# Expert stage: order of the gate eviction's access, one gate group moved from ACT to DVE, row rates, last squares added on DVE

## The chip, the cores and the metric

The kernel runs on one core of a Trainium2 chip. Its engines work side by side, each on its own queue in order: PE (TensorE, matrix products), DVE (VectorE), ACT (ScalarE), POOL (GpSimd) and SP (it only issues DMA transfers). They wait for one another through semaphores. The metric is the device time of one execution in microseconds (us); lower is better.

## The reference, cut to what matters

Two transformer blocks run one after the other on 512 tokens of width 1024. The change touches the last part of the first block, a mixture of 16384 experts:

```python
def block(xb):                       # 128 tokens
    q = (xb @ w_q).reshape(PEER_BLOCK, PEER_HEADS, 2, PEER_QDIM // 2)
    s = jnp.einsum('thsd,hsnd->thsn', q, sub_keys)
    sv, si = lax.top_k(s, PEER_TOPK)
    ...
    top, pos = lax.top_k(cand, PEER_TOPK)
    e = jnp.take_along_axis(cidx, pos, axis=-1)   # 8 heads x 16 experts a token
    g = jax.nn.softmax(top, axis=-1)
    act = jax.nn.gelu(jnp.einsum('thkd,td->thk', u_tab[e], xb), approximate=False)
    return jnp.einsum('thk,thkd->td', g * act, v_tab[e])
```

Each token uses 128 of the 16384 rows of the up-table `u_tab` and the down-table `v_tab`. The result is added to the block's `h`, and the next block begins with a root-mean-square norm of `h`.

## The kernel before, in words

Products are done in full fp32 precision as three products of two-part operands (`mm3`, L167 to L169): high times high, high times low, low times high. Weights come in blocks of 1 MB (`wload`) and are cut into halves of 1024 columns; `halves` makes the high part on ACT (L119, tile `whi`) and the low part on DVE by a subtraction (L120, tile `wlo`). Activations are split in the same way: L161 on ACT and L162 on DVE with a gain, L158 and L159 without.

The expert stage (`experts`) treats the tokens in two ways.

- The first 128 tokens fetch their own table rows. `gathered` is a generator of steps: an indirect DMA on POOL's queue (L1005) fetches one row for each of 128 tokens, 0.52 MB, and one DVE instruction works on an earlier row: a dot product with a row of the up-table (`dot`, L1010) or a weighted addition of a row of the down-table (`add`, L1021). There are 256 rows. `some(n)` takes n such steps on average; `RATE` holds n for the first 28 units, for the other units, and for each half of a down-table block. Each step is tied to a recent matrix product, so that it doesn't run ahead of PE.
- The other 384 tokens multiply with the whole tables. `unit(b)` loads one block of the up-table (b from 0 to 63), runs 48 products of 384 columns each three times, and evicts with the Gelu on ACT (L1252). Sixty units stand in a first loop; their results go to DRAM (`act_dram`).

Beside the units of the first loop runs `side`, a generator whose parts are taken up by cost (`DUE` for each unit): `select` (choice of experts, on DVE) and `gates`. `gates` makes, for 16 tokens at a time, a tile `st` with the gate of every expert. A group is four tokens. It needs a one-hot matrix `ga` scaled by the gate and a one-hot matrix `gb` (L1212, DVE). For three of four groups `ga` is a comparison on DVE (L1202) and four scalings on ACT (L1204); for the fourth it is four Abs (L1207) and four Relu (L1209) on ACT. Four matrix products (L1190) give a PSUM tile of four tokens by 128, and `finish` evicts it on ACT into `st` (L1191). A full tile goes to DRAM (`gate_dram`).

A second loop runs over 16 blocks c of four units, in the order 0, 15, 1 to 14. `read` fetches the activations of a block from DRAM, or `evaluate` runs the last four units for block 15. `weigh` loads the gates (L1283, tile `gt`, POOL's queue) and multiplies them in on DVE (L1287, tile `wt`), with a split by L158 and L159. `combine` multiplies with the down-table of the block before. So `evaluate(15)` and `weigh(15)` are issued ahead of the first `combine`: this place is called "between the tables" below. After the last block `done(m)` splits `h` for the next stage and adds up its squares (`sq_add`: a Square on ACT, an addition L200 on POOL).

The order of each engine's queue is set by a scheduler from this program; nothing is written out by hand.

Of the kernel before, what the change touches and what calls it, by code (L numbers as in the profile page):

```python
# [15 lines left out]
AF = mybir.ActivationFunctionType  # L16
ALU = mybir.AluOpType
# [5 lines left out]
T = 512  # L23
# [16 lines left out]
ON_POOL = (2, 3, 4, 5, 6, 7)  # L40
GATHERED = 128
PACE, PACE_D, AHEAD_G = 2, 4, 1
RATE = (0.9, 2.6, 2.2)
OHB, UGB = 1, 6
ULAG = 1
FIRST, STEP = (6, 3, 3), (1, 1, 1)
# [6 lines left out]
class Kern:  # L53
# [130 lines left out]
        return y  # L184


    def sq_add(self, acc, src, first, n=T, eng=None):
        nc = self.nc
        if eng is not None and first:
            eng.tensor_mul(acc[:, :n], src, src)  # L190
        elif eng is not None:
            sq = self.t(self.sp, [P, T], "sq")
            eng.tensor_mul(sq[:, :n], src, src)
            nc.gpsimd.tensor_add(acc[:, :n], acc[:, :n], sq[:, :n])
        elif first:
            nc.scalar.activation(acc[:, :n], src, AF.Square)
        else:
            sq = self.t(self.sp, [P, T], "sq")
            nc.scalar.activation(sq[:, :n], src, AF.Square)  # L199
            nc.gpsimd.tensor_add(acc[:, :n], acc[:, :n], sq[:, :n])  # L200

    def acc_rstd(self, acc, width, n=T):
        nc = self.nc
# [779 lines left out]
    def experts(self, ctx):  # L983


        nc, A, tc, gv = self.nc, self.A, self.tc, self.gv
# [61 lines left out]
        def some(n):  # L1048
            pace.append(self.last_mm)
            credit[0] += n  # L1050
            while credit[0] >= 1:
                credit[0] -= 1
                next(rows, None)

        with tc.tile_pool(name="pa", bufs=1) as sp_, ExitStack() as es:
# [22 lines left out]
            with tc.tile_pool(name="pq", bufs=2) as qp:  # L1078
                rb = self.bcast(self.norm()[1](), qp, "rb")
                for k in range(KD):  # L1080
                    t = self.t(qp, [P, T], "xt", bufs=KD)
# [102 lines left out]
            def gates(tt):  # L1184
                late = []

                def finish(st, t0, a, bs):
                    ps = self.ps()
                    for i in range(4):
                        nc.tensor.matmul(ps[:, i * P:(i + 1) * P], bs[:, i, :], a[:, i, :], start=True, stop=True)  # L1190
                    nc.scalar.activation(st[:, :, t0:t0 + 4].rearrange("p i t -> p t i"), ps.rearrange("p (t i) -> p t i", t=4), AF.Copy)  # L1191

                for tb in range(max(tt * P - G, 0) // TG, (tt * P + P - G) // TG):
                    st = self.t(ap, [P, P, TG], "st", bufs=2)
                    for t0 in range(0, TG, 4):
                        t = tb * TG + t0
                        a = self.t(ap, [P, 4, P], "ga", bufs=LAG + 2)
                        four = lambda n: picks[n][:, t:t + 4, None].to_broadcast([P, 4, P])
                        rows4 = iota[:, None, :].to_broadcast([P, 4, P])

                        if t0 // 4 % 4 != 3:
                            nc.vector.tensor_tensor(a, rows4, four(0), op=ALU.is_equal)  # L1202
                            for i in range(4):
                                nc.scalar.activation(a[:, i, :], a[:, i, :], AF.Copy, scale=picks[2][:, t + i:t + i + 1])  # L1204
                        else:
                            for i in range(4):
                                nc.scalar.activation(a[:, i, :], iota, AF.Abs, bias=picks[0][:, t + i:t + i + 1], scale=-1.0)  # L1207
                            for i in range(4):
                                nc.scalar.activation(a[:, i, :], a[:, i, :], AF.Relu, bias=picks[2][:, t + i:t + i + 1],  # L1209
                                                     scale=picks[3][:, t + i:t + i + 1])  # L1210
                        bs = self.t(ap, [P, 4, P], "gb", bufs=LAG + 1)
                        nc.vector.tensor_tensor(bs, rows4, four(1), op=ALU.is_equal)  # L1212
                        late.append((st, t0, a, bs, tb))
                        if len(late) > LAG:
                            z = late.pop(0)
                            finish(*z[:4])
                            if z[1] == TG - 4:
                                nc.scalar.dma_start(gate_d[z[4]], z[0].rearrange("p i t -> p (i t)"))
                        yield GCOST[tt]
                for z in late:  # L1220
                    finish(*z[:4])
                    if z[1] == TG - 4:
                        nc.scalar.dma_start(gate_d[z[4]], z[0].rearrange("p i t -> p (i t)"))
                    yield 0.1
# [30 lines left out]
            while b < 60 or b < 64 and work is not None or b % 4:  # L1255
# [11 lines left out]
                if room:  # L1267
                    some(RATE[0 if b < 28 else 1])
            for _ in work or ():
                pass  # L1270
        first = b // 4
        with tc.tile_pool(name="pb", bufs=2) as ap:
            def slots():
                while True:
                    yield self.t(ap, [P, D], "ug", bufs=UGB)
            room["u"] = slots()

            def weigh(c, acts, pool, tag):

                W = []  # L1280
                for b0 in range(0, 8, 4):
                    gt = self.t(ap, [P, N // TG, 4, TG], "gt", bufs=3)
                    nc.gpsimd.dma_start(gt.rearrange("p b i t -> p b (i t)"),  # L1283
                                        gate_d[:, :, (c * 8 + b0) * TG:(c * 8 + b0 + 4) * TG].rearrange("b j c -> j b c"))
                    for b in range(b0, b0 + 4):
                        w = self.t(ap, [P, N], "wt", bufs=2)
                        nc.vector.tensor_mul(w.rearrange("p (b t) -> p b t", t=TG), acts(b).rearrange("p (b t) -> p b t", t=TG), gt[:, :, b - b0, :])  # L1287
                        h, l = self.split(w, n=N, tag=tag, pool=pool, bufs=8)
                        W.append((h[:, :N], l[:, :N]))
                return W  # L1290

            acc = []

            def combine(c, W, begin, end):

                for dh in range(2):
                    if end and dh == 0:
                        for _ in rows:
                            pass
                    if begin:  # L1300
                        acc.extend(self.ps()[:, :N] for _ in range(4))
                    for sub in range(2):
                        v = self.wload(A["peer_v"][c, dh, sub])
                        for e0 in range(0, 4, 2):
                            for d in range(4):
                                for e in range(e0, e0 + 2):
                                    k = sub * 4 + e
                                    self.mm3(acc[dh * 4 + d], v(e * 512 + d * P, e * 512 + (d + 1) * P), W[k], begin and k == 0, end and k == 7)
                        if end and dh == 1 and sub == 0:
                            for k0 in (0, 4):  # L1310
                                gathered_out(k0)
                            for m in range(4):
                                self.done(m)
                        some(RATE[2])
                    if end:
                        for m in range(dh * 4, dh * 4 + 4):
                            nc.vector.tensor_add(self.hT[m][:, G:], acc[m], self.hT[m][:, G:])
                            if dh == 1:
                                self.done(m)

            def read(c):
                ac = [self.t(ap, [P, 2, 2, N], "ac", bufs=3) for _ in range(2)]
                for b in range(2):
                    nc.gpsimd.dma_start(ac[b].rearrange("p b a t -> p b (a t)"), act_d[c * 4 + 2 * b:c * 4 + 2 * b + 2].rearrange("b j c -> j b c"))
                return ac

            def evaluate(c):
                ac = [self.t(ap, [P, 2, 2, N], "ac", bufs=3) for _ in range(2)]
                for b in range(4):
                    unit(c * 4 + b, ac[b // 2][:, b % 2])  # L1330
                    some(RATE[1])
                return ac


            order, W = [0, *range(first, 16), *range(1, first)], None
            for i, c in enumerate(order):
                ac = evaluate(c) if c >= first else read(c)
                W2 = weigh(c, lambda b: ac[b // 4][:, b % 4 // 2, b % 2, :], *((self.xp, "x") if i % 2 else (ap, "w")))
                if W is not None:
                    combine(order[i - 1], W, i == 1, False)  # L1340
                W = W2
            combine(order[-1], W, False, True)


# [551 lines left out]
```

## Time and profile before

| quantity | value |
|---|---|
| median of three runs | 4026.0 us (4025.2 to 4029.67) |
| the profiled execution, its own time | 4027.37 us |
| span of its trace, first to last instruction | 4025.5 us |
| mean granted clock of PE | 0.983 |
| busy, share of the span | PE 97%, DVE 61%, ACT 43%, POOL 19% |

The span is 1.9 us shorter than the time of that execution. [...] The expert stage lies at about 495 to 1856 us: the query product up to 610, the units without gates to about 735, units with gates to 1258, the place between the tables to about 1292, the down-table to 1836, and then the next stage, whose first instructions overlap with its end.

### The profile page before, as it was taken

To read this page: it belongs to the slowest core of one execution; us is meant where nothing else is said; L and a number is where in the kernel's file an instruction comes from. 1 tells how busy PE (TensorE), PEld (TensorE's weight loads), DVE (VectorE), ACT (ScalarE), POOL (GpSimd) and SP (SyncE) were. 2 spreads that over 40 slices of the span, in tenths; PEclk is the share of its full clock that TensorE was granted. 3 is DMA by queue.
4 is the path that set the end of the run, shared out by engine and by line. 5 is a ranking of instruction groups with operands and counts; after the bars stand their busy time and mean duration, and the time that the engine had idled before them with its cause. 6 is when DMAs were issued, how large, how long until landed. Compare 5 with 4: busy or idle time off the path is not lost.

```text
span 4025.5 us, 52157 instructions
## 1 busy us (share of the span) xinstructions
PE 3903.0 (97%) x20105; PEld 3426.6 (85%) x20105; DVE 2466.5 (61%) x4683; ACT 1730.9 (43%) x3040; POOL 745.9 (19%) x704
## 2 busy tenths in 40 slices
PE   7999999899998999999999999999999999999999
PEld 6878789899988999998888778888888888888887
DVE  7666459988766788876444575643444447665443
ACT  3445434567774333333223365532332236654222
POOL 7401100122323555542000101000000011010000
PEclk8989999999998999999999999999999999999999
DMA  4214225578977999983223211222222232032232
GB/s 138 69 37 136 74 74 177 202 269 289 329 273 273 359 385 357 355 311 128 97 97 101 92 43 63 85 91 102 92 102 99 95 97 69 32 105 74 89 105 79
DMA packets 130042, 608.27 MB, mean 151 GB/s; under 512 B 22320, under 2 KB 25568, under 8 KB 89472
## 3 DMA queue, kind: packets, MB, share of 16 engines
q1 hardware_dynamic: 55296, 362.96, 25.6%
q0 software_dynamic: 48672, 185.73, 13.1%
q10 hardware_dynamic: 25824, 56.23, 3.9%
q8 instruction: 158, 2.59, 0.3%
q14 instruction: 92, 0.75, 0.1%
HBM read 551.92 MB, written 52.95 MB: 150 GB/s over the span
## 4 chain that ended last, share of the span: by engine, by line
PE 80%; DVE 11%; ACT 3%; DMA 2%; issue 1%; POOL 1%; SPq 0%; ACTq 0%; DVEq 0%; POOLq 0%
PE ps_ffn L168 12%; PE ps_ffn L167 12%; PE ps_ffn L169 12%; PE ps_peer L169 7%; PE ps_peer L167 7%; PE ps_peer L168 7%; PE ps_mixer L168 2%; PE ps_mixer L167 2%; PE ps_mixer L169 2%; DVE wlo_peer L120 2%; PE ps_peer L1190 1%; DMA gt_peer<-gate_dram 1%; PE ps_xm L167 1%; PE ps_mem L167 1%; PE ps_xm L169 1%
## 5 line engine op out<-in xcount | busy, mean ns | idle before, releaser
L119 ACT ACTIVATE whi_ffn<-wraw_ffn 128x1024 fp32r<-128x1024 f32 (+2 forms) x304 | 278.7, 944 | 924.2 <-PE ps_ffn L168 906.4
L167 PE MATMUL ps_peer<-xh_peer,whi_peer 128*128 128x384 f32 (+1 forms) x1664 | 578.0, 348 | 28.2 <-ACT whi_peer L119 26.0
L169 PE MATMUL ps_peer<-xh_peer,wlo_peer 128*128 128x384 f32 (+1 forms) x1664 | 570.9, 344 | 12.5 <-DVE wlo_peer L120 12.2
L168 PE MATMUL ps_peer<-xl_peer,whi_peer 128*128 128x384 f32 (+1 forms) x1664 | 570.7, 343 | 0.0
L119 ACT ACTIVATE whi_peer<-wraw_peer 128x1024 fp32r<-128x1024 f32 x272 | 286.1, 1056 | 435.1 <-PE ps_peer L168 409.6
L120 DVE TENSOR_TENSOR wlo_ffn<-wraw_ffn,whi_ffn 128x1024 fp32r<-128x1024 f32 (+2 forms) x304 | 331.0, 1090 | 180.6 <-ACT whi_ffn L119 179.9
L120 DVE TENSOR_TENSOR wlo_peer<-wraw_peer,whi_peer 128x1024 fp32r<-128x1024 f32 x272 | 330.2, 1222 | 120.3 <-ACT whi_peer L119 104.3
L331 DVE TENSOR_TENSOR g_ffn<-ps_ffn,rb_ffn 128x512 f32<-128x512 f32 x88 | 60.8, 691 | 480.4 <-PE ps_ffn L169 480.4
L167 PEld LDWEIGHTS ps_peer<-xh_peer,whi_peer 128*128 128x128 f32 x1664 | 318.2, 191 | 38.1 <-ACT whi_peer L119 30.9
L169 PEld LDWEIGHTS ps_peer<-xh_peer,wlo_peer 128*128 128x128 f32 x1664 | 317.5, 191 | 22.4 <-DVE wlo_peer L120 16.8
L168 PEld LDWEIGHTS ps_peer<-xl_peer,whi_peer 128*128 128x128 f32 x1664 | 318.0, 191 | 4.7
L167 PE MATMUL ps_ffn<-xh_xm,whi_ffn 128*128 128x512 f32 x704 | 274.2, 390 | 0.0
L169 PE MATMUL ps_ffn<-xh_xm,wlo_ffn 128*128 128x512 f32 x704 | 273.9, 389 | 0.0
L168 PE MATMUL ps_ffn<-xl_xm,whi_ffn 128*128 128x512 f32 x704 | 273.9, 389 | 0.0
L167 PE MATMUL ps_ffn<-ah_ffn,whi_ffn 128*128 128x512 f32 x704 | 273.9, 389 | 0.0
L168 PE MATMUL ps_ffn<-al_ffn,whi_ffn 128*128 128x512 f32 x704 | 273.9, 389 | 0.0
L169 PE MATMUL ps_ffn<-ah_ffn,wlo_ffn 128*128 128x512 f32 x704 | 273.9, 389 | 0.0
L200 POOL TENSOR_TENSOR sqacc_ffn<-sqacc_ffn,sq_ffn 128x512 f32<-128x512 f32 x21 | 30.6, 1456 | 1039.3 <-ACT sq_ffn L199 1033.1
L169 PE MATMUL ps_peer<-wh_peer,wlo_peer 128*128 128x384 f32 x512 | 171.9, 338 | 14.0 <-DVE wlo_peer L120 14.0
L167 PE MATMUL ps_peer<-wh_peer,whi_peer 128*128 128x384 f32 x512 | 171.7, 335 | 0.0
L168 PE MATMUL ps_peer<-wl_peer,whi_peer 128*128 128x384 f32 x512 | 171.6, 335 | 0.0
L1005 POOL DMA_INDIRECT ug_peer<-in_peer_v_rows_dram,idx_peer x85 | 135.9, 1598 | 128.0 <-DVE accg_peer L1021 59.2
(762 smaller groups left out, 9258.8 us busy)
## 6 DMA issues: line engine op xcount, KB each, us to landing
wraw_ffn<-in_ffn_gu_dram SPq DMA_DIRECT2D x88, 1024.0 KB, 4.7
wraw_peer<-in_peer_u_dram SPq DMA_DIRECT2D x64, 1024.0 KB, 5.6
wraw_peer<-in_peer_v_dram SPq DMA_DIRECT2D x64, 1024.0 KB, 8.1
wraw_ffn<-in_ffn_dn_dram SPq DMA_DIRECT2D x64, 704.0 KB, 4.0
gate_dram<-st_peer ACTq DMA_DIRECT2D x24, 1024.0 KB, 7.4
gt_peer<-gate_dram POOLq DMA_DIRECT2D x32, 768.0 KB, 11.2
act_dram<-at_peer ACTq DMA_DIRECT2D x60, 384.0 KB, 4.3
ac_peer<-act_dram POOLq DMA_DIRECT2D x30, 768.0 KB, 8.6
```

Source lines behind the costliest of these rows:

```text
L119: nc.scalar.activation(hi[:, :m], raw, AF.Copy)
L120: nc.vector.tensor_sub(lo[:, :m], raw, hi[:, :m].bitcast(F32))
L167: nc.tensor.matmul(ps, a[0], b[0], start=first, stop=False)
L168: nc.tensor.matmul(ps, a[0], b[1], start=False, stop=False)
L169: nc.tensor.matmul(ps, a[1], b[0], start=False, stop=last)
L200: nc.gpsimd.tensor_add(acc[:, :n], acc[:, :n], sq[:, :n])
L331: nc.vector.tensor_mul(g, pg, rb)
L1005: nc.gpsimd.indirect_dma_start(out=u, out_offset=None, in_=A[table], in_offset=bass.IndirectOffsetOnAxis(ap=idx[:, s:s + 1], axis=0))
L1190: nc.tensor.matmul(ps[:, i * P:(i + 1) * P], bs[:, i, :], a[:, i, :], start=True, stop=True)
```

## The change

Five edits, all in the expert stage.

- `RATE` goes from (0.9, 2.6, 2.2) to (0.6, 3.0, 2.3): fewer rows in the first 28 units, more in the others and in the down-table.
- The gate eviction in `finish` copies the same 128x512 elements, but runs through them in the order of its target. Before, it read PSUM in order and wrote each element 64 bytes from the one before; now it writes `st` in runs of four elements and reads PSUM in steps of 512 bytes.
- For the second and third gate sets (`tt` over 1), the fourth group's `ga` is made on DVE by a comparison and a multiplication instead of eight instructions on ACT.
- `evaluate` takes no rows.
- At the end of the stage, `done` doesn't add the squares; `sq_add` does it after the splits of each half, with the addition on DVE.

```diff
--- before.py
+++ after.py
@@ -40,7 +40,7 @@
 ON_POOL = (2, 3, 4, 5, 6, 7)
 GATHERED = 128
 PACE, PACE_D, AHEAD_G = 2, 4, 1
-RATE = (0.9, 2.6, 2.2)
+RATE = (0.6, 3.0, 2.3)
 OHB, UGB = 1, 6
 ULAG = 1
 FIRST, STEP = (6, 3, 3), (1, 1, 1)
@@ -184,20 +184,21 @@
         return y
 
 
-    def sq_add(self, acc, src, first, n=T, eng=None):
+    def sq_add(self, acc, src, first, n=T, eng=None, add=None):
         nc = self.nc
+        add = add or nc.gpsimd
         if eng is not None and first:
             eng.tensor_mul(acc[:, :n], src, src)
         elif eng is not None:
             sq = self.t(self.sp, [P, T], "sq")
             eng.tensor_mul(sq[:, :n], src, src)
-            nc.gpsimd.tensor_add(acc[:, :n], acc[:, :n], sq[:, :n])
+            add.tensor_add(acc[:, :n], acc[:, :n], sq[:, :n])
         elif first:
             nc.scalar.activation(acc[:, :n], src, AF.Square)
         else:
             sq = self.t(self.sp, [P, T], "sq")
             nc.scalar.activation(sq[:, :n], src, AF.Square)
-            nc.gpsimd.tensor_add(acc[:, :n], acc[:, :n], sq[:, :n])
+            add.tensor_add(acc[:, :n], acc[:, :n], sq[:, :n])
 
     def acc_rstd(self, acc, width, n=T):
         nc = self.nc
@@ -1188,7 +1189,7 @@
                     ps = self.ps()
                     for i in range(4):
                         nc.tensor.matmul(ps[:, i * P:(i + 1) * P], bs[:, i, :], a[:, i, :], start=True, stop=True)
-                    nc.scalar.activation(st[:, :, t0:t0 + 4].rearrange("p i t -> p t i"), ps.rearrange("p (t i) -> p t i", t=4), AF.Copy)
+                    nc.scalar.activation(st[:, :, t0:t0 + 4], ps.rearrange("p (t i) -> p i t", t=4), AF.Copy)
 
                 for tb in range(max(tt * P - G, 0) // TG, (tt * P + P - G) // TG):
                     st = self.t(ap, [P, P, TG], "st", bufs=2)
@@ -1198,7 +1199,10 @@
                         four = lambda n: picks[n][:, t:t + 4, None].to_broadcast([P, 4, P])
                         rows4 = iota[:, None, :].to_broadcast([P, 4, P])
 
-                        if t0 // 4 % 4 != 3:
+                        if tt > 1 and t0 // 4 % 4 == 3:
+                            nc.vector.tensor_tensor(a, rows4, four(0), op=ALU.is_equal)
+                            nc.vector.tensor_mul(a, a, four(2))
+                        elif t0 // 4 % 4 != 3:
                             nc.vector.tensor_tensor(a, rows4, four(0), op=ALU.is_equal)
                             for i in range(4):
                                 nc.scalar.activation(a[:, i, :], a[:, i, :], AF.Copy, scale=picks[2][:, t + i:t + i + 1])
@@ -1310,13 +1314,16 @@
                             for k0 in (0, 4):
                                 gathered_out(k0)
                             for m in range(4):
-                                self.done(m)
+                                self.done(m, False)
+                                self.sq_add(self.acc, self.hT[m], m == 0, add=nc.vector)
                         some(RATE[2])
                     if end:
                         for m in range(dh * 4, dh * 4 + 4):
                             nc.vector.tensor_add(self.hT[m][:, G:], acc[m], self.hT[m][:, G:])
                             if dh == 1:
-                                self.done(m)
+                                self.done(m, False)
+                        for m in range(4 * dh, 8 * dh):
+                            self.sq_add(self.acc, self.hT[m], False, add=nc.vector)
 
             def read(c):
                 ac = [self.t(ap, [P, 2, 2, N], "ac", bufs=3) for _ in range(2)]
@@ -1328,7 +1335,6 @@
                 ac = [self.t(ap, [P, 2, 2, N], "ac", bufs=3) for _ in range(2)]
                 for b in range(4):
                     unit(c * 4 + b, ac[b // 2][:, b % 2])
-                    some(RATE[1])
                 return ac
```

On ACT, in the later units with gates, the rows of one stretch before (L1191 is the eviction, L1204 the scaling, L1207 and L1209 the fourth group, L1252 the Gelu):

```order
L1191 ACTIVATE st_peer_9640<-ps_peer_10045 128x4x128
L1258 DMA act_dram<-at_peer_9972 128x768
L1191 ACTIVATE st_peer_9640<-ps_peer_10067 128x4x128
L1191 ACTIVATE st_peer_10036<-ps_peer_10082 128x4x128
L1218 DMA gate_dram<-st_peer_9640 128x2048
L1204 ACTIVATE ga_peer_10074<-ga_peer_10074,pick_peer_5180 128x128 x4
L1252 ACTIVATE at_peer_10097<-ps_peer_10108 128x384
L1207 ACTIVATE ga_peer_10161<-iota_peer_5176,pick_peer_5178 128x128 x4
L1209 ACTIVATE ga_peer_10161<-ga_peer_10161,pick_peer_5180,pick_peer_5181 128x128 x4
L1204 ACTIVATE ga_peer_10192<-ga_peer_10192,pick_peer_5180 128x128
```

And the matching stretch of the changed kernel, where L1192 is the eviction and L1208 the scaling:

```order
L1192 ACTIVATE st_peer_9601<-ps_peer_10006 128x128x4
L1262 DMA act_dram<-at_peer_9933 128x768
L1192 ACTIVATE st_peer_9601<-ps_peer_10028 128x128x4
L1192 ACTIVATE st_peer_9997<-ps_peer_10043 128x128x4
L1222 DMA gate_dram<-st_peer_9601 128x2048
L1208 ACTIVATE ga_peer_10035<-ga_peer_10035,pick_peer_5180 128x128 x4
L1256 ACTIVATE at_peer_10058<-ps_peer_10069 128x384
L1208 ACTIVATE ga_peer_10147<-ga_peer_10147,pick_peer_5180 128x128 x4
L119 ACTIVATE whi_peer_10179<-wraw_peer_10173 128x1024
L119 ACTIVATE whi_peer_10288<-wraw_peer_10286 128x1024
```

The eviction has its two inner dimensions exchanged, and the eight instructions of the fourth group are gone, so that a copy of weights (L119) follows the scalings.

On DVE, between the tables, the last twelve rows up to the first subtraction for the down-table, `wlo_peer_12026`; L1010 and L1021 are the row instructions:

```order
L159 TENSOR_TENSOR wl_peer_11679<-wt_peer_11676,wh_peer_11678 128x384
L1021 SCALAR_TENSOR_TENSOR accg_peer_4356<-ug_peer_11749,act_peer_4359,accg_peer_4356 128x1024
L1010 SCALAR_TENSOR_TENSOR ug_peer_11752,hid_peer_4358<-ug_peer_11752,xg_peer_4355 128x1024
L1021 SCALAR_TENSOR_TENSOR accg_peer_4356<-ug_peer_11817,act_peer_4359,accg_peer_4356 128x1024
L1010 SCALAR_TENSOR_TENSOR ug_peer_11820,hid_peer_4358<-ug_peer_11820,xg_peer_4355 128x1024
L1021 SCALAR_TENSOR_TENSOR accg_peer_4356<-ug_peer_11885,act_peer_4359,accg_peer_4356 128x1024
L1015 TENSOR_TENSOR act_peer_4359<-act_peer_4359,g_peer_4360 128x16
L1010 SCALAR_TENSOR_TENSOR ug_peer_11890,hid_peer_4358<-ug_peer_11890,xg_peer_4355 128x1024
L1021 SCALAR_TENSOR_TENSOR accg_peer_4356<-ug_peer_11893,act_peer_4359,accg_peer_4356 128x1024
L1010 SCALAR_TENSOR_TENSOR ug_peer_11958,hid_peer_4358<-ug_peer_11958,xg_peer_4355 128x1024
L1021 SCALAR_TENSOR_TENSOR accg_peer_4356<-ug_peer_11961,act_peer_4359,accg_peer_4356 128x1024
L120 TENSOR_TENSOR wlo_peer_12026<-wraw_peer_12023,whi_peer_12025 128x1024
```

The same place in the changed kernel, where the multiplication is L1291 and the first subtraction for the down-table is `wlo_peer_11918`:

```order
L159 TENSOR_TENSOR wl_peer_11588<-wt_peer_11585,wh_peer_11587 128x384
L159 TENSOR_TENSOR wl_peer_11594<-wt_peer_11591,wh_peer_11593 128x384
L1291 TENSOR_TENSOR wt_peer_11597<-ac_peer_11554,gt_peer_11583 128x384
L1291 TENSOR_TENSOR wt_peer_11603<-ac_peer_11554,gt_peer_11583 128x384
L159 TENSOR_TENSOR wl_peer_11600<-wt_peer_11597,wh_peer_11599 128x384
L1291 TENSOR_TENSOR wt_peer_11861<-ac_peer_11609,gt_peer_11859 128x384
L120 TENSOR_TENSOR wlo_peer_11918<-wraw_peer_11915,whi_peer_11917 128x1024
L159 TENSOR_TENSOR wl_peer_11606<-wt_peer_11603,wh_peer_11605 128x384
L1291 TENSOR_TENSOR wt_peer_11867<-ac_peer_11609,gt_peer_11859 128x384
L120 TENSOR_TENSOR wlo_peer_11922<-wraw_peer_11915,whi_peer_11921 128x1024
```

No row instruction stands ahead of the subtraction any more; the first multiplication of block 15, which needs the gate tile `gt_peer_11859`, does. On POOL's queue the loads of `gt_peer_11859` and its neighbour now follow the loads for block 0 at once, where eleven row transfers stood before them.

On DVE, at the end of the stage, before (L162 splits `h`, L1317 adds the expert result to `h`, `wlo_ffn` belongs to the next stage):

```order
L162 SCALAR_TENSOR_TENSOR xl_peer_16940<-h_91,gains,xh_peer_16939 128x512
L1317 TENSOR_TENSOR h_92<-ps_peer_12151,h_92 128x384
L120 TENSOR_TENSOR wlo_ffn_3191_17048<-wraw_ffn_3187_17041,whi_ffn_3190_17047 128x1024
L162 SCALAR_TENSOR_TENSOR xl_peer_17006<-h_92,gains,xh_peer_17005 128x512
L1317 TENSOR_TENSOR h_93<-ps_peer_12152,h_93 128x384
L1317 TENSOR_TENSOR h_94<-ps_peer_12153,h_94 128x384
L1317 TENSOR_TENSOR h_95<-ps_peer_12154,h_95 128x384
L120 TENSOR_TENSOR wlo_ffn_3200_17124<-wraw_ffn_3198_17121,whi_ffn_3199_17123 128x1024
L162 SCALAR_TENSOR_TENSOR xl_peer_17014<-h_93,gains,xh_peer_17013 128x512
L162 SCALAR_TENSOR_TENSOR xl_peer_17022<-h_94,gains,xh_peer_17021 128x512
L162 SCALAR_TENSOR_TENSOR xl_peer_17030<-h_95,gains,xh_peer_17029 128x512
```

And in the changed kernel, where L1322 adds the result and L201 adds the squares:

```order
L162 SCALAR_TENSOR_TENSOR xl_peer_16844<-h_91,gains,xh_peer_16843 128x512
L201 TENSOR_TENSOR sqacc_peer_16823<-sqacc_peer_16823,sq_peer_16847 128x512
L1322 TENSOR_TENSOR h_92<-ps_peer_12046,h_92 128x384
L1322 TENSOR_TENSOR h_93<-ps_peer_12047,h_93 128x384
L120 TENSOR_TENSOR wlo_ffn_3189_16948<-wraw_ffn_3187_16945,whi_ffn_3188_16947 128x1024
L162 SCALAR_TENSOR_TENSOR xl_peer_16910<-h_92,gains,xh_peer_16909 128x512
L162 SCALAR_TENSOR_TENSOR xl_peer_16915<-h_93,gains,xh_peer_16914 128x512
L1322 TENSOR_TENSOR h_94<-ps_peer_12048,h_94 128x384
L1322 TENSOR_TENSOR h_95<-ps_peer_12049,h_95 128x384
L201 TENSOR_TENSOR sqacc_peer_16823<-sqacc_peer_16823,sq_peer_16928 128x512
L162 SCALAR_TENSOR_TENSOR xl_peer_16920<-h_94,gains,xh_peer_16919 128x512
L162 SCALAR_TENSOR_TENSOR xl_peer_16925<-h_95,gains,xh_peer_16924 128x512
```

Two additions of squares stand among these rows, and the second subtraction for the next stage now comes after the last split instead of before the split of `h_92`.

## Rows read from the trace of the kernel before

**Rows 1.** Windows: microseconds, then busy time (and instructions) of each engine, clock, DMA.
```profile
735.00:921.00 186.00, 173.30 (x1047) 170.95 (x1047) 167.97 (x479) 130.56 (x265) 39.57 (x26) 0.96 0.69 242
921.00:1258.00 337.00, 314.00 (x1910) 309.68 (x1909) 236.66 (x301) 245.14 (x505) 91.08 (x70) 0.96 0.80 286
1258.00:1312.00 54.00, 41.95 (x229) 41.20 (x228) 34.74 (x49) 17.12 (x29) 27.58 (x23) 0.87 0.89 319
1312.00:1415.00 103.00, 97.36 (x555) 95.77 (x554) 83.04 (x119) 37.54 (x53) 54.82 (x39) 1.00 0.94 355
750.00:850.00 100.00, 90.92 (x552) 89.17 (x551) 99.42 (x342) 70.86 (x140) 14.56 (x8) 0.97 0.56 195
```

**Rows 2.** PE's waits in the windows of rows 1 and 1835–1870: total, times, longest.
```profile
PE ps_peer L169 <- DVE wlo_peer L120: 6.1, 4, 2.0
PE ps_peer L167 <- ACT whi_peer L119: 4.9, 1, 4.9
...
PE ps_peer L167 <- ACT whi_peer L119: 20.3, 10, 5.0
...
PE ps_peer L169 <- DVE wlo_peer L120: 12.0, 1, 12.0
...
PE ps_peer L169 <- DVE wlo_peer L120: 4.8, 3, 2.1
...
PE ps_ffn L168 <- DVE xl_peer L162: 3.2, 2, 2.5
```

**Rows 3.** Timeline of ACT before one gap: start, length, instructions.
```profile
1219.21 1.60 ACT L1209 ACTIVATE ga_peer<-ga_peer,pick_peer,pick_peer 128x128 f32<-128x128 f32 x4
...
1221.54 1.25 ACT L1204 ACTIVATE ga_peer<-ga_peer,pick_peer 128x128 f32<-128x128 f32 x4
...
1223.53 2.00 ACT L119 ACTIVATE whi_peer<-wraw_peer 128x1024 fp32r<-128x1024 f32 x2
```

**Rows 4.** Timeline of PE after that gap: first, 16th and 26th step.
```profile
1224.64 0.69 PE L167 MATMUL ps_peer<-xh_peer,whi_peer 128*128 128x384 f32 x1 [4.83 <-ACT whi_peer L119]
...
1229.91 0.39 PE L169 MATMUL ps_peer<-xh_peer,wlo_peer 128*128 128x384 f32 x1
...
1231.71 0.33 PE L168 MATMUL ps_peer<-xl_peer,whi_peer 128*128 128x384 f32 x1
```

**Rows 5.** Groups of ACT by line, 921–1258: busy time, mean ns, idle before.
```profile
L1191 ACT ACTIVATE st_peer<-ps_peer 128x512 f32<-128x512 f32 x65 | 68.9, 1078 | 4.7 <-ACT st_peer L1191 2.1 <-PE ps_peer L1190 1.4 <-ACT ga_peer L1207 0.2
...
L1209 ACT ACTIVATE ga_peer<-ga_peer,pick_peer,pick_peer 128x128 f32<-128x128 f32 x64 | 26.8, 483 | 0.0
L1207 ACT ACTIVATE ga_peer<-iota_peer,pick_peer 128x128 f32<-128x128 f32 x64 | 20.3, 388 | 0.0
```

**Rows 6.** The contiguous copy L1105: ns (shortest, median, longest), first and last start.
```profile
L1105 ACT ACTIVATE xn_peer<-ps_peer x16: 577/582/622, 516.9 to 608.6; 128x512 f32<-128x512 f32 x16
```

**Rows 7.** Groups of DVE by line, 921–1258, as rows 5.
```profile
L1021 DVE SCALAR_TENSOR_TENSOR accg_peer<-sc_peer,act_peer,accg_peer 128x1024 f32<-128x1024 f32 x38 | 48.7, 1281 | 38.3 <-PE ps_peer L169 38.2
L1010 DVE SCALAR_TENSOR_TENSOR sc_peer<-sc_peer,xg_peer 128x1024 f32<-128x1024 f32 x37 | 45.2, 1222 | 28.6 <-PE ps_peer L169 28.6
L1212 DVE TENSOR_TENSOR gb_peer<-iota_peer,pick_peer 128x512 f32<-128x512 f32 x62 | 42.3, 690 | 1.8 <-PE ps_peer L1190 1.8
```

**Rows 8.** Timeline of DVE between the tables: first, last row instruction, subtractions after.
```profile
1288.29 1.22 DVE L1010 SCALAR_TENSOR_TENSOR ug_peer<-ug_peer,xg_peer 128x1024 f32<-128x1024 f32 x1
...
1301.62 1.28 DVE L1021 SCALAR_TENSOR_TENSOR accg_peer<-ug_peer,act_peer,accg_peer 128x1024 f32<-128x1024 f32 x1 [0.60 <-DMA ug_peer<-in_peer_v_rows_dram,idx_peer]
1302.82 2.35 DVE L120 TENSOR_TENSOR wlo_peer<-wraw_peer,whi_peer 128x1024 fp32r<-128x1024 f32 x2
```

**Rows 9.** DVE's waits in 1258–1312.
```profile
DVE wt_peer L1287 <- DMA gt_peer<-gate_dram: 7.1, 1, 7.1
```

**Rows 10.** The split L162 in other stages and at this end, as rows 6.
```profile
L162 DVE SCALAR_TENSOR_TENSOR xl_ffn<-h,gains,xh_ffn x24: 744/747/747, 2161.9 to 3314.0; 128x512 fp32r<-128x512 f32 x24
...
L162 DVE SCALAR_TENSOR_TENSOR xl_peer<-h,gains,xh_peer x8: 740/1756/1780, 1838.9 to 1854.6; 128x512 fp32r<-128x512 f32 x8
```

## Prediction

> **What bounds the kernel now.** I read the table of windows first, because the change touches only the expert stage, and a share over the whole kernel would say little about it. In that table the reader is to compare PE's busy time with the length of its window [rows 1]. PE is busy for nearly all of each window, so a shorter time can come only from PE's idle time and from the time that its clock was at the lower of its two levels. In 921 to 1258 us, the stretch in which gate tiles are made beside the up-table, PE is idle for 337 − 314.0 = 23.0 us at a mean granted clock of 0.96. In 735 to 921 us it is idle for 12.7 us, also at 0.96. Between the two tables (1258 to 1312) it is idle for 12.1 us at 0.87, and in the first part of the down-table (1312 to 1415) for 5.6 us at 1.00.
>
> The waits of PE say who ended these gaps [rows 2]. In 921 to 1258 it is ACT's copy of the weights, L119 (20.3 us in 10 waits). In 735 to 921 it is that copy (4.9) and DVE's subtraction L120 (6.1). Between the tables one wait on L120 takes all 12.0 us, three more take 4.8 in the next window, and at the stage's end two waits on the split L162 take 3.2.
>
> ACT is busy for only 245 of the 337 us, so it is late in bursts, not on the whole. The timeline before one such gap shows a burst [rows 3]: four L1209 (1.60 us), four L1204 (1.25), with evictions between, and the copy L119 that PE waits for begins at 1223.53, behind all of them. PE starts again at 1224.64 after 4.83 us, and then runs slowly: 15 steps to 1229.91 take 5.27 us, 0.35 each, and the next ten to 1231.71 take 0.18 each [rows 4]. [...]
>
> **The change part by part.** The sum is made against the profiled execution, 4027.4 us, which is 1.4 above the median of the three.
>
> *ACT in the gate stage.* In 921 to 1258 ACT ran 64 L1207 (20.3 us) and 64 L1209 (26.8 us), that is 16 groups of four tokens, and 65 gate evictions L1191 of 1078 ns [rows 5]. All of these 16 groups go to DVE: −47.1 us. The eviction has 128x512 elements on either side of the change; what changes is which side has gaps, the write before and the PSUM read after. No row shows a read of PSUM with gaps. The bounds are 0.58 us, the same size copied with no gaps by L1105 [rows 6], and 1.08, that the read costs what the write did. I take 0.60: both ends are rows of the same engine, size and source, and the one difference of L1191 from L1105 is its pattern. Where the runs of four now lie in the write, the write is near to L1105's. That is 65 × 0.48 = −31 us. ACT then works 245 − 47 − 31 = 167 us, half of the window, and the burst of [rows 3] shrinks by the 1.6 us of L1209, as much of L1207 before it, and 0.48 for each of its evictions.
>
> [...]
>
> How much PE wins: the idle 20.3 us, and the time lost at the low clock. For the latter the clock gives bounds: 0.04 × 337 × 2 = 27 us at the lower level, of which between 23 (every idle us) and none was idle, so 2 to 13.5 us were lost by half-speed work; the shown gap lost 2.6 of them for 4.83 idle. I take 8, the middle. Of 28.3 us I count 85%, since ACT still has groups of L1204 ahead of L119: **−24** (bounds 0 and −28.3).
>
> *735 to 921 us.* The same edits touch the later part, and the row rate of 0.6 in place of 0.9 takes row work from DVE there. Lost at low clock by the same reading: 1.1 to 7.4, taken 4. DVE's part remains half open, because 750 to 850 has DVE busy for 99.4 of 100 us with expert selection, which is not touched [rows 1]. Half of 12.7 + 4: **−8.3** (bounds 0 and −16.7).
>
> *DVE and DMA in the gate stage.* DVE gets two instructions for each of the 16 groups, at the 690 ns of L1212, an operation of the same kind and size: +22 us. The rate of 3.0 for 2.6 is 0.4 more rows in each of some 30 units: +12 × 1.25 (L1010 and L1021, 1222 and 1281 ns) = +15 us [rows 7]. Against 237 us that gives 274 us, in a window of about 337 − 28 = 309: 89%. That is still under full, but its bursts have less room. The nearest row is 750 to 850, where DVE is full and PE idles 9.1 us in 100, with perhaps 3 lost at the 0.97 clock: 12 per 100 us. At 89% I take a quarter of that over 3.1 hundreds: **+8.5** (bounds 0 and 33).
>
> *No rows between the tables.* DVE runs one queue in order. Before, five dots and five adds of rows stand in it from 1288.29 to 1302.82, and the subtraction L120 that ends PE's 12.0 us begins behind them [rows 8]. They are gone from that place. What stands there now is the multiplication L1291 for the next block, which needs the third gate load. A gate load cost DVE 7.1 us of waiting here [rows 9]; the third is issued right behind the second without rows between, so I take it as hidden by the 16 multiplications and splits of the first two, and keep 7.1 us as the bound if it isn't. The ten take some 13 of these 14.5 us, a little more than PE waited; without them L120 ends at about the moment PE asks for it, so 0.6 us may stay. The clock of 0.87 over 54 us makes 14 us at the low level, of which 1 to 7 were lost by half-speed work; after one gap it was 2.6 [rows 4], so I take 2. Sum 12.0 + 2 − 0.6: **−13.4** (bounds −6 and −14).
>
> *Down-table.* The rate of 2.3 for 2.2 and the rows that moved out of the middle balance the 7 rows that are done earlier, so nothing changes in the steady part, where PE never waits. Of the 4.8 us after the middle I count what follows from DVE's backlog there, **−2** (0 to −5.6).
>
> *End of the stage.* Seven additions leave POOL for DVE, and the splits come ahead of some of them. L162 took 747 ns in other stages and 1756 at the median here, where POOL's additions run beside it [rows 10]. [...] Some five of the eight splits get 1.0 us each back and seven additions of 0.69 cost 4.8, but only three of them stand before the last split that PE needs; the second subtraction of the next stage's weights now stands behind that split and may cost 1 us of wait. Of 3.2 us idle and an estimated 1.5 at the low clock, less than after the longer gap of [rows 4]: **−3** (0 to −4.7).
>
> Sum: −24 − 8.3 + 8.5 − 13.4 − 2 − 3 = −42.2, so 3985.2 on the profiled time, and 1.4 less, 3984, on the median.
>
> **The rivals.** *The eviction stays at 1.08.* ACT is then relieved by 47 us and not by 78, three fifths; the gate stage gives −14.4 and the window before −6: 3996. For it speaks that no row shows the read; against it that ACT would still lose the longest single piece of its bursts.
>
> *DVE takes ACT's place.* If it stops PE over the whole stretch as it does in 750 to 850, but with the clock half as costly, 10.6 per 100 us, that is +33 in place of +8.5: 4008. For it: 89%, and the one-hot groups come in bursts. Against it: 67 us of DVE's idle time there is the paced rows' waiting for PE, which is room [rows 7].
>
> *Rows come late, the slower side.* Each row's dot and add stand in DVE's queue ahead of L120, so a late row stops PE. Rows, weights and gate tiles moved 286 GB/s over 337 us, 96.4 MB; with 12 rows of 0.52 MB more in 309 us it would be 332 GB/s. In 921 to 1258 the dots and adds waited for PE alone, but at 319 GB/s the last add waited 0.60 us for its row [rows 1, 7, 8]. About 87 such instructions are due after the change. DVE's room is 309 − 274 = 35 us; lateness beyond it stops PE, in place of the 8.5. At a mean of 0.6 us, 52 us, the time is 3984 − 8.5 + 17 = 3993. It decides from a mean of about 1.1 us: 96 − 35 = 61, 4036. Against it: 355 GB/s is held in the down-table.
>
> *It doesn't do what it says.* PE's gaps in the gate stage end with ACT's copy only because that came last, with DVE's L120 just behind it, and between the tables a gate load takes the place of the rows. Then the two gate windows give nothing and the middle only 6; with the 2 behind it that is 4027.4 − 8 = 4019, 4018 on the median. For it: L120 follows L119 on each block, so it can be late by nearly as much. Against it: DVE had 100 us without work in that stretch.
>
> **How the numbers follow.** The sum 0.52 (own range 3968 to 3993); slow eviction 0.15; DVE in ACT's place 0.14; late rows past their point 0.06; waits that only change their owner 0.08 (at the edge of no change); more gained than the sum, all bounds at their good end, 0.05. A change under 0.2%, about 8 us, can't be told from none by a measurement of this kernel. From the cases: faster 0.84, same 0.09, slower 0.07. The good end of all bounds is 4026 − 28.3 − 16.7 − 14 − 5.6 − 4.7 = 3957. The range leaves out the late rows and the upper half of the cases near no change, and reaches from 3962 to 4014.
>
> **What would show it.** In the changed profile: the gate eviction near 0.60 us (or 1.08: first rival); waits of PE on L119 in the gate stage down from 20.3 to under 6; DVE above 85% busy there, with waits of PE on L120 as the price; a gap between the tables under 2 us, or one that ends with a gate load; splits at the end near 0.75 us. The prediction is wrong if PE waits for L120 in the gate stage for more than 20 us, or DVE waits for row loads there.

## The result and the profile after

The changed kernel takes 3964.4 us (median) against 4026.1 before: ratio 0.9845, 95% interval 0.9831 to 0.9859. That is 62 us less where the prediction had 42, inside its range (3962 to 4014) and at its fast end. The profiled execution took 3964.74 us, with a span of 3963.0 and a mean clock of 0.988.

The five stretches of the changed kernel that answer to [rows 1]:

```profile
734.00:918.50 184.50, 172.83 (x1048) 170.24 (x1047) 161.53 (x450) 119.17 (x266) 32.90 (x25) 0.96 0.67 241
918.50:1221.50 303.00, 300.40 (x1912) 300.21 (x1912) 268.20 (x355) 179.99 (x377) 116.39 (x82) 1.00 0.93 340
1221.50:1257.00 35.50, 35.50 (x207) 35.50 (x205) 23.27 (x37) 16.71 (x30) 16.58 (x14) 1.00 0.88 316
1257.00:1360.00 103.00, 100.63 (x577) 99.67 (x577) 85.46 (x119) 37.69 (x52) 57.24 (x42) 1.00 0.98 375
749.00:848.00 99.00, 90.87 (x556) 88.90 (x555) 97.89 (x321) 64.98 (x141) 8.41 (x5) 0.97 0.53 184
```

The second row, the gate stage, is the main result. The same PE work (1912 instructions for 1910) takes 303 us for 337. PE's idle time went from 23.0 to 2.6 us, and its busy time from 314.0 to 300.4: with 20.4 us of waiting had come 13.6 more of busy time, at a mean granted clock of 0.96 for 1.00 now. The clock records of both traces hold two values, 1.00 and 0.50. Before, this stretch has six pieces at 0.50, 23.9 us together, each begun 3.3 to 5.0 us after the start of one of PE's waits; around the gap of [rows 4] the clock is 1.00 in 1222 to 1223 us, 0.50 in 1224 to 1230 and 1.00 again from 1231. At 0.50 the steps of [rows 4] take 0.35 us for 0.18, so half of the 23.9, 11.9 us, is the most that half speed cost; what the rest of the 13.6 is isn't shown. The first and the last row show what didn't move: 734 to 918 us keeps 11.7 idle us. PE's waits in the first two stretches and in the fourth, as [rows 2] (in the third there is none):

```profile
PE ps_peer L169 <- DVE wlo_peer L120: 6.9, 5, 2.0
PE ps_peer L167 <- ACT whi_peer L119: 3.2, 2, 3.0
...
PE ps_peer L169 <- DVE wlo_peer L120: 2.6, 1, 2.6
...
PE ps_peer L169 <- DVE wlo_peer L120: 2.3, 2, 1.3
```

The 20.3 us on L119 in the gate stage are gone, and so is the 12.0 between the tables; the 2.6 on L120 stood there before as well. Three more rows: the eviction (now L1192), in ACT's groups of 918 to 1221 us as in [rows 5]; the wait of DVE for a gate load as in [rows 9]; and the split at the stage's end as in [rows 10]:

```profile
L1192 ACT ACTIVATE st_peer<-ps_peer 128x512 f32<-128x512 f32 x64 | 37.4, 592 | 5.7 <-PE ps_peer L1191 3.7 <-issue 1.4
```

```profile
DVE wt_peer L1291 <- DMA gt_peer<-gate_dram: 2.9, 1, 2.9
```

```profile
L162 DVE SCALAR_TENSOR_TENSOR xl_peer<-h,gains,xh_peer x8: 737/744/747, 1783.0 to 1793.2; 128x512 fp32r<-128x512 f32 x8
```

Matching points of both traces (the issue of each unit's result; the product at the end of the row accumulation, 1836.3 before and 1780.8 now) divide the 62.5 us of span: 1.1 up to 735 us, 1.4 to 921, 34.3 to 1258, 18.7 to 1836 (place between the tables and down-table), 7.0 at the end.

### The profile page after: what moved, and what is told of

Same layout as the page of the kernel before. It is cut to its first block, busy times and chain, and to the rows that moved or that the text cites. A ratio compares the mean times of both kernels' runs of the same rounds, so it can differ in the third digit from the quotient of the medians.

```text
span 3963.0 us, 52091 instructions
## 1 busy us (share of the span) xinstructions
PE 3881.0 (98%) x20105; PEld 3411.8 (86%) x20105; DVE 2481.3 (63%) x4722; ACT 1653.2 (42%) x2912; POOL 735.6 (19%) x697
## 4 chain that ended last, share of the span: by engine, by line
PE 86%; DVE 9%; ACT 2%; POOL 1%; issue 1%; DMA 1%; SPq 0%; DVEq 0%; ACTq 0%; POOLq 0%
PE ps_ffn L169 12%; PE ps_ffn L167 12%; PE ps_ffn L168 12%; PE ps_peer L169 8%; PE ps_peer L167 8%; PE ps_peer L168 8%; PE ps_mixer L168 2%; PE ps_mixer L167 2%; PE ps_mixer L169 2%; PE ps_peer L1191 2%; PE ps_xm L167 1%; PE ps_mem L167 1%; PE ps_xm L169 1%; DVE wlo_peer L120 1%; PE ps_mem L168 1%; PE ps_xm L168 1%
## 5 line engine op out<-in xcount | busy, mean ns | idle before, releaser
L119 ACT ACTIVATE whi_ffn<-wraw_ffn 128x1024 fp32r<-128x1024 f32 (+2 forms) x304 | 278.8, 944 | 920.0 <-PE ps_ffn L168 916.7
L119 ACT ACTIVATE whi_peer<-wraw_peer 128x1024 fp32r<-128x1024 f32 x272 | 286.6, 1056 | 441.1 <-PE ps_peer L168 410.7
L120 DVE TENSOR_TENSOR wlo_ffn<-wraw_ffn,whi_ffn 128x1024 fp32r<-128x1024 f32 (+2 forms) x304 | 329.4, 1085 | 181.7 <-ACT whi_ffn L119 181.0
L120 DVE TENSOR_TENSOR wlo_peer<-wraw_peer,whi_peer 128x1024 fp32r<-128x1024 f32 x272 | 329.8, 1219 | 99.5 <-ACT whi_peer L119 83.6
L201 POOL TENSOR_TENSOR sqacc_ffn<-sqacc_ffn,sq_ffn 128x512 f32<-128x512 f32 x21 | 30.6, 1457 | 1058.1 <-ACT sq_ffn L200 1051.9
L168 PEld LDWEIGHTS ps_ffn<-al_ffn,whi_ffn 128*128 128x128 f32 x704 | 132.2, 188 | 27.5
```

Of the source, the lines that this page charges most:

```text
L119: nc.scalar.activation(hi[:, :m], raw, AF.Copy)
L120: nc.vector.tensor_sub(lo[:, :m], raw, hi[:, :m].bitcast(F32))
L168: nc.tensor.matmul(ps, a[0], b[1], start=False, stop=False)
L201: add.tensor_add(acc[:, :n], acc[:, :n], sq[:, :n])
```

## The experiments

Each edit is to the changed kernel, unless it says otherwise; times are medians. The changed kernel wasn't run again beside each of them. The kernel before was, with medians of 4023.1 to 4027.2 us, so a difference of up to some 4 us between two of these kernels says nothing by itself.

**E1, the eviction's order undone.**

```diff
-nc.scalar.activation(st[:, :, t0:t0 + 4], ps.rearrange("p (t i) -> p i t", t=4), AF.Copy)
+nc.scalar.activation(st[:, :, t0:t0 + 4].rearrange("p i t -> p t i"), ps.rearrange("p (t i) -> p t i", t=4), AF.Copy)
```

> The changed kernel with only the gate eviction back in its old order (gaps in the write to st, PSUM read in order). My theory: PE lost time in the gate stage because ACT's bursts made the weight copy L119 late, and each gap cost once more by the lower clock after it; the eviction is one part of the bursts. ACT gets 64 x 0.49 = 31 us back between 918 and 1221 us (180 to 211 of 303), so waits of PE on L119 should return in part: 5 to 10 us idle and about two thirds of that lost at the lower clock, time 3973 to 3981. Rival A, the groups moved to DVE did it alone: no change, 3964 within 3. Rival B, this edit is the whole gain of the gate stage: 34 us back, 3998.

3964.2 us. Rival A took it: the eviction takes 1099 ns again, ACT works about 204 us for 180 in the gate stage, and nothing is lost.

**E2, the groups back on ACT.**

```diff
-if tt > 1 and t0 // 4 % 4 == 3:
+if tt > 9 and t0 // 4 % 4 == 3:
```

> The changed kernel with only the fourth groups of the second and third gate sets back on ACT (Abs and Relu). My theory: 16 groups are 47 us of ACT (180 to 227 of 303) and 22 us less on DVE, and the four Abs and four Relu stand in one piece; waits of PE on L119 return: 6 to 14 us idle, with the lower clock 10 to 23, time 3974 to 3987. Rival A, the eviction's order did it alone: 3964 within 3, or a little less since DVE gets 22 us of room. Rival B, this edit is the whole gain of the gate stage: 3998.

4012.5 us, 48 more: above each case. The gate stage, and PE's waits in it:

```profile
917.00:1264.00 347.00, 320.39 (x1909) 313.56 (x1908) 249.81 (x322) 221.56 (x506) 115.02 (x82) 0.94 0.82 296
```

```profile
PE ps_peer L167 <- ACT whi_peer L119: 19.2, 9, 4.0
PE ps_peer L169 <- DVE wlo_peer L120: 7.4, 7, 2.7
```

That is 24 us more idle than in the changed kernel, and 20 more busy at a clock of 0.94. It costs more than the same groups did before (34). Here PE waits 7.4 us for L120, where it was 2.6 before, and there are six long gaps for five (the table below); how much is due to each isn't shown.

**E5, the same ACT work without Abs and Relu.** Old eviction, and the fourth group as the others:

```diff
-nc.vector.tensor_mul(a, a, four(2))
+for i in range(4):
+    nc.scalar.activation(a[:, i, :], a[:, i, :], AF.Copy, scale=picks[2][:, t + i:t + i + 1])
```

> The changed kernel with the old order of the gate eviction and with the fourth groups of the last two gate sets made as the other three are: comparison on DVE, four scalings on ACT. ACT's work between 918 and 1221 us is then 180 + 23 + 16 x 1.2 = 222 us, as much as the 222 that it had with Abs and Relu in the run in which the groups were back on ACT (4012 us). Theory of load (which the second run seemed to bear out): the same ACT work gives the same waits, about 4005 to 4012. Theory of place: Abs and Relu need nothing from DVE or PE, so they are put into ACT's queue ahead of weight copies, and it is this place and not ACT's total that makes PE wait; scalings wait for DVE's comparison and stand elsewhere: under 3 us of waits on L119, 3964 to 3970.

3965.6 us, and no wait on L119:

```profile
918.50:1221.50 303.00, 300.41 (x1908) 299.84 (x1907) 257.11 (x337) 221.74 (x440) 119.41 (x81) 1.00 0.93 340
```

ACT has 221.7 us of work here and 221.6 in E2, and the loss is all in one of them. So ACT's load is not the cause. The order of its queue is. Each half-unit of products needs one copy of weights L119 and ends with one Gelu on ACT. I counted for every Gelu how many copies L119 for later half-units stand ahead of it in ACT's queue. With none, PE must finish its half-unit, the Gelu must wait for that, and only then comes the next copy, behind whatever else is queued. In the later gate units (Gelus 60 to 117; E13 and E6 follow below):

```
kernel         none ahead at Gelu number      gaps of PE on L119 over 1.5 us, at
before         67, 95, 101, 107, 113          959, 1108, 1146, 1186, 1225
E2             69, 77, 95, 101, 107, 113      967, 1014, 1111, 1152, 1191, 1232
E13            69, 77                         966, 1013
changed, E1, E5, E6                none       none
```

The other runs have no such place in these units and no such gap. Each place has its gap: Gelu 113 belongs to unit 56, whose result was issued at 1217.9 before, and the gap follows at 1224.64 [rows 4]. ACT's row for this Gelu before, which stands ahead of the first of [rows 3], and for Gelu 113 of the changed kernel with the row ahead of it:

```profile
1217.40 0.49 ACT L1252 ACTIVATE at_peer<-ps_peer 128x384 f32<-128x384 f32 x1 [1.86 <-PE ps_peer L169]
...
1187.92 1.06 ACT L119 ACTIVATE whi_peer<-wraw_peer 128x1024 fp32r<-128x1024 f32 x1 [1.67 <-PE ps_peer L168]
1188.88 0.47 ACT L1256 ACTIVATE at_peer<-ps_peer 128x384 f32<-128x384 f32 x1
```

Before, ACT sat idle for 1.86 us until PE had finished the half-unit, and the next copy came at 1223.53. In the changed kernel a copy stands ahead of the Gelu. One more such place in the first gate set (Gelu 37 before, 41 now) has the gap at 794, now at 812. Why the scheduler leaves no copy ahead at just these Gelus isn't shown; in the second and third gate set it does so only where their fourth groups are Abs and Relu.

**E13, only the second set's groups back on ACT** (`tt > 2` in that line).

> The changed kernel with the fourth groups of the second gate set back on ACT and those of the third on DVE: half of the 41 us of ACT work that cost 48 us when all of it was back. Theory of place: what counts is how often a Gelu stands in ACT's queue with no weight copy ahead of it beyond those that PE has used; in the later units this is so 6 times with all groups on ACT, twice here and never in the changed kernel, so 2 gaps on L119, and 48 x 2/6 = 16 us: 3976 to 3983. Theory of load: half of the work, half of the loss, 3986 to 3990, with gaps spread over all groups of that set.

3980.4 us, two gaps, as the count has it. The issue of each unit's result shows where the time went: compared with the changed kernel, E13 falls back by 14.6 us from unit 33 to unit 39, around the two gaps, by 1.2 more up to unit 48, and by nothing after that.

**E6, before with the groups' edit alone** (`if tt > 1 and t0 // 4 % 4 == 3:` with its two DVE instructions).

> The kernel before with only the fourth groups of the second and third gate sets moved to DVE. If that edit alone frees the gate stage: 34 us less than before, 3990 to 3994, with the gaps between the tables and at the stage's end as before. If it needs the new row rates or the eviction's order too: 4005 to 4020.

3992.6 us, 31 less than before measured beside it (4023.1), with no wait on L119 after 921. This edit alone frees the gate stage, at the old rates and the old eviction.

**E3, rows between the tables** (`some(RATE[1])` in `evaluate` again).

> The changed kernel with rows again in the four units between the two tables. My theory: the dots and adds stand in DVE's queue ahead of the subtraction that PE needs for the first block of the down-table, so a gap of 10 to 14 us on L120 returns there with 2 to 7 us at the lower clock behind it; fewer rows are left for the down-table, whose steady part has no waits to lose: 3976 to 3984. Rival, the gap was the wait for the gate load (7.1 us before, 2.9 now): the gap stays away, 3964 within 3.

3987.3 us: 23 more. The gap is back: PE waits 7.8 us for L120 at 1262, and in DVE's queue five dots and five adds of rows, from 1246.3 on, stand ahead of that subtraction. Later gaps of 2.7, 3.0 and 5.1 come at 1316, 1347 and 1438, where the changed kernel has 1.3 at most. Ahead of these DVE had waited 2.6, 3.5 and 9.9 us for gate loads, and then worked on rows before the late subtraction; why they come isn't shown.

**E11, the end as before** (`done(m)` with its squares on POOL), and **E4, only the additions on POOL** (without `add=nc.vector`).

> The changed kernel with the end of the stage as before: squares right behind each split, additions on POOL. The end lost 3.7 us of waits before, and the whole end was 6.5 to 7 us longer: theory 3970 to 3971. The additions on POOL in the new place cost 2.4, so 4 of these are the place. Rival, the end's gain came from DVE being less behind when the down-table ends: 3964 to 3967.

> The changed kernel with the seven last additions of squares on POOL again, in their new place behind the splits. My theory: the splits and subtractions on DVE slow down beside POOL's additions (L162 from 0.70 to about 1.7 us), PE waits 2 to 4 us for them and loses as much at the lower clock: 3968 to 3971. Rival, the place of the splits ahead of the squares is what counted, not the engine: 3964 within 1.5.

3969.6 and 3966.8 us: 5.2 more for the whole end, and 2.4 for the engine, which the times alone can't tell from nothing. The traces add that in E4 the slowest split still takes 1778 ns (the median 744) and PE waits 1.5 us for a split; in E11 the median split takes 1542 and PE waits 3.2.

**E7, E8, E10, the row rates** (0.6, 3.7, 2.3), (0.9, 2.6, 2.2) and (0.2, 3.0, 2.7) for (0.6, 3.0, 2.3).

> The changed kernel with a rate of 3.7 rows in place of 3.0 in the later units. DVE gets 0.7 x 30 x 1.25 = 26 us more in the gate stage, 268 to 294 of 303 (97%). My prediction's price for a nearly full DVE was 12 us per 100: by it 10 to 30 us more, 3975 to 3995. Rival, late rows: the transfers reach 340 + 36 = 376 GB/s and DVE waits for rows: also slower, but with waits on row loads named. Rival, DVE's queue bears it: the 22 rows missing from the down-table change nothing either, 3964 within 3.

> The changed kernel with the row rates of before. Theory: the rates only move rows that nothing waits for, now that the gate stage has no burst on ACT; the down-table gets some 7 rows more in stretches where PE never waits: 3964 within 4, or up to 3968 through the waits on L120 at the start of the down-table. Rival, the early rate matters in 735 to 918 us, where DVE is full: 0.3 rows more in some 14 units is 5 us more DVE work, 3969 to 3975.

> The changed kernel with row rates of 0.2, 3.0 and 2.7 for 0.6, 3.0 and 2.3: some 11 rows leave the first 28 units for the down-table. If DVE's row work is what makes PE wait in 735 to 918 (11.7 us idle, 8 us more at the lower clock at most): 7 us less DVE work there, 3956 to 3962. Rival, the down-table has no room for 2.7 rows in half a block: waits on L120 there, 3968 to 3980. If selection alone fills DVE there: 3964 within 3.

3975.9, 3973.1 and 3974.9 us. In E7 rows come late, as in the slower rival; DVE's waits in its gate stage name them:

```profile
DVE sc_peer L1011 <- DMA sc_peer<-in_peer_u_rows_dram,idx_peer: 3.9, 1, 3.9
...
DVE accg_peer L1022 <- DMA sc_peer<-in_peer_v_rows_dram,idx_peer: 2.4, 2, 1.8
```

But late rows are only a part of its loss. At 366 GB/s and with DVE busy for 294 of 313.5 us, PE waits 7.6 us for L120 in two waits. The shorter, 2.5 at 1092, follows two of these waits for rows (3.9 and 1.8). The longer, 5.1 at 930, follows DVE's own work, which ran without a pause from 918 to the late subtraction.

E8 loses some 5 us up to the last unit and the rest at the end, where rows are left over (its last add stands at 1793 us, for 1764 in the changed kernel) and PE waits 4.3 us in small pieces. E10 wins nothing in 734 to 918, though DVE works 10 us less there (PE is idle for 11.3 us), and pays 7.4 us of waits in the down-table.

**E9, no Abs and Relu in the first gate set either.**

```diff
-elif t0 // 4 % 4 != 3:
+elif tt == 1 or t0 // 4 % 4 != 3:
```

> The changed kernel with the fourth groups of the first gate set made as the other three are (comparison on DVE, scalings on ACT), so that no Abs and Relu are left. Theory of place: the one gap on L119 that the changed kernel still has (3.2 us at 812) comes from a Gelu of that set that stands in ACT's queue with no weight copy ahead of it; by the order of the queues this place goes away, 3 to 6 us less with the clock, 3958 to 3962. Rival, DVE is the bound in 749 to 848 (99% busy): 7 comparisons of 0.69 us more make PE wait for L120 instead, 3964 to 3970.

3955.2 us (ratio to before 0.9825, 0.9811 to 0.9838): the fastest of all. The last place without a copy ahead is gone, and the two windows, and the one that answers to 749 to 848, read

```profile
734.00:911.00 177.00, 170.51 (x1039) 169.37 (x1038) 163.71 (x450) 107.83 (x240) 29.70 (x25) 0.96 0.68 247
911.00:1214.00 303.00, 303.00 (x1928) 303.00 (x1928) 269.79 (x355) 177.39 (x372) 120.40 (x82) 1.00 0.94 344
749.00:848.00 99.00, 99.00 (x630) 98.79 (x629) 98.83 (x325) 63.28 (x138) 8.28 (x7) 1.00 0.61 219
```

DVE has eight comparisons more to do, though it was full there. In 749 to 848 it is busy for 98.8 of 99 us, and PE doesn't wait at all; one wait of 2.9 us on L120 follows at 852.

## Why the prediction was right, and where not

The time lies in the range, but the sum was 20 us short. 3964.4 lies between the sum's own range (3968 to 3993) and the case of more gained than the sum (3957), which had 0.05. That it is inside is owed to the 6 us by which the stated range reached beyond the sum's own, and to two terms whose errors nearly cancel (−8.3, measured −1.4, and +8.5, measured 0): that much is luck. Where most would be won was right: the gate stage, then the place between the tables. The reason given for the gate stage was only half right: that ACT's copies came late behind other work was so, but the length of this work didn't matter.

- *ACT in the gate stage, −24.* Measured −34.3, all of it here. The size had two errors: PE's busy time fell by 13.6 us, where I had chosen 8 for half-speed work (at most 11.9 of it by the clock; the gap that I took for a measure lost 15 steps × 0.17 = 2.6 us), and the gaps went entirely, not by 85%. The reason had one: "the burst shrinks by" work taken off ACT. The eviction was as short as I said (592 ns for 0.60) and was worth nothing (E1). What the gaps hung on is the place of the copies in ACT's queue (E5, E13), and the groups' edit alone moved them (E6). The timeline around [rows 3] had it: the Gelu at 1217.40 stands ahead of these rows, with no copy before it. I read the length of that burst, not its order. No row of before showed a read of PSUM with gaps; the changed eviction reads in steps of 512 bytes and takes 592 ns, where L1105, which reads in order, takes 582 [rows 6].
- *734 to 918 us, −8.3.* Measured −1.4. The half that I gave to ACT and the lower row rate didn't come: one queue place without a copy stayed, and L120 waits 6.9 us for 6.1. I had called the stretch bound by DVE and priced it as half open. E10 shows that less DVE work there wins nothing, and E9 that some 6 us of it hung on Abs and Relu in ACT's queue (by the issue of the unit results E9 is 1.7 us ahead of the changed kernel at 735 us and 7.7 at 919).
- *DVE's load, +8.5.* Measured 0. DVE is busy for 268 of 303 us, 88.5% as worked out (89%), with no new wait of PE and no wait of DVE for a row load. The price by 750 to 850 was wrong, since that stretch's gaps were not DVE's alone: in E9 DVE is as full and PE doesn't wait. (A quarter of 12 per 100 us over 3.1 hundreds is also 9.3, not 8.5.) In E7, at 94% and 366 GB/s, the loss is there; where it begins between the two wasn't tried.
- *Between the tables and down-table, −13.4 and −2.* Together −18.7: the gap went entirely, the gate load's 2.9 us stayed hidden, and idle time in the first part of the down-table fell from 5.6 to 2.4 us. E3 bears out the mechanism with the gap of 7.8 us behind ten row instructions; the rest of its 23 us falls later.
- *End, −3.* Measured −7.0 between the traces, 5.2 by E11. Before, five of the eight splits ran beside additions on POOL (L200) for 1.2 us or more and took 1.75 to 1.78 us; the one at 1847.99, beside which POOL sat idle for all but the last 0.4 us, took 0.74. Now POOL adds nothing there and all eight take 0.74 to 0.75. Both waits on the split went; the additions of squares (0.68 us each) fitted among the splits without a wait of PE.

The terms that were too small (ACT, down-table, end) and the price for DVE that didn't come outweigh the one that was too large (734 to 918 us). The slow eviction, DVE in ACT's place and unmoved waits didn't come true; late rows exist, but at higher rates.

## What to carry to other kernels

When PE waits in gaps for an engine that has time left, look up in that engine's queue what stands ahead of the late instruction, and count the places, before summing its work: 42 us more or less on ACT changed nothing here, and six places in its queue cost 48 us. Work that only fills gaps (the rows) should be kept out of the place where another stage begins (23 us here, E3). Its rate matters too: each of three other settings cost 9 to 12 us, or 10 to 14 by the ratio to the kernel before.

## What was not expected of the hardware

A wait of PE cost much more than its length: 20.4 us idle came with 13.6 us more of busy time in the gate stage (clock 0.96 for 1.00), and 24 with 20 in E2 (0.94). In E13 the stretch around two gaps of 2.4 and 2.9 us lost 14.6 (clock 0.98 over its gate stage). Why the ratio differs between the runs, by the number of gaps or by their place, wasn't tried.
